# Sample attention as a chain of steps beside the prompt's weight tiles, and sixteen feed-forward tiles for the prompt alone

## The chip, the core and the metric

The kernel runs on one core of a Trainium2 chip. The core has a matrix engine (PE), whose weights are loaded by a second stream of instructions (PEld), a vector engine (DVE, VectorE), a scalar engine (ACT, ScalarE), a general engine (POOL, GpSimd) and SyncE (SP), which here only issues transfers. Each engine takes its instructions in the order of its own queue and waits on semaphores. Sixteen DMA engines carry the transfers that the queues of SP, ACT and POOL issue. PE writes its results to PSUM, eight banks of 128 x 512 float32, from where DVE or ACT fetch them; everything else lives in SBUF.

The metric is the time of one execution in microseconds (us) on the device. The kernel before was timed three times: 1074.62 us in the median, 1070.83 to 1075.09.

## The reference

One layer of a decoder handles a prompt of 512 rows and, with the same weights, 32 rows of samples (8 sequences of 4 new tokens), all of 1024 features in float32:

```python
h = rmsnorm(x, norm_mix_g)
q, k, v, qi, ki, wi, xl, gl, ga, gb = split_cols(h @ w_in, IN_SPLITS)
y_a = attend(q, k, v, qi, ki, wi) @ w_proj_a          # 8 heads of 64
y_b = (rg_lru(conv(xl)) * gelu(gl)) @ w_proj_b
x = x + (sigmoid(ga) * y_a + sigmoid(gb) * y_b) @ w_out
h = rmsnorm(x, norm_ffn_g)
ua, ub = split_cols(h @ w_up, (D_FF, D_FF))           # D_FF = 3072
uc = causal_dwconv(ua, width 3)
x = x + (gelu(uc) * ub) @ w_down
```

`attend` for a sample row scores 4096 past positions with a small indexer, takes the best 256, and attends to those alone: their keys and values (2 KB a row each) lie in a paged cache, so that each of the 32 rows gathers 256 rows of keys and 256 of values, at places that are known only at run time. The softmax also takes in the new tokens of the same sequence. Outputs are the normed rows, new keys and values, and states.

## The kernel before, in words

*Precision and weights.* Products that need it are made of float32r pairs: `load_w` (L162) loads a weight tile of 512 KB on SP's queue into one of three buffers `wr`; ACT makes the high half `wh` (L167), DVE the low half `wl` (L168), two buffers of each. A product then is three matmuls, high with high, low with high, high with low.

*The order of the work.* The program is written as a list; a planner with its own simulated timeline puts it into one queue for each engine. `tc.high_priority(n)` moves a part ahead in its choice, and `tc.issue_after(x)` allows an instruction only behind x. It is free otherwise, and the queues it makes are fixed: on the chip an instruction that waits holds all behind it in its engine's queue.

*Stages.* The first part, up to about 420 us, does the indexer, the recurrent block and the prompt's attention. Then come the choice of the samples' rows (L845 to L894), the projection of the prompt's attention (`w_proj_a`, L990 to L1010) and `w_out` (L1019 to L1044). The choice writes `idx`, the lists of 2 x 128 cache rows for each of the 32 sample rows.

*The feed-forward part for the prompt alone* (L1247 to L1265). D_FF is cut into 24 tiles of 128. The first NP = 12 are computed for the prompt's 512 columns alone with `form_p` (L253): two products (for `ua` and `ub`) of 24 matmuls of 512 columns each, the convolution on DVE, gelu on ACT, the halves `Gh` and `Gl`. After each four tiles `form_a` (L215) adds their part of `w_down`: 2 x 48 matmuls of 512 columns.

*The samples' attention* (L1059 to L1222) stands beside it in the list, at a priority of its own, so that the planner mixes both. `gather` (L1059) issues two indirect transfers of 256 KB on POOL's queue for a sample row, behind the last norm (`normed`); there are six buffers `cg` for them. Three ways turn 256 keys into scores, by a letter in `WAYS` (L147): with D (17 rows) DVE multiplies by the broadcast query (L1118; the query comes by an ACT-issued transfer of 256 KB) and sums in groups of 64 (L1125); with A (5 rows) DVE multiplies and ACT sums by 16 instructions (L1122); with P (10 rows) PE turns the keys by eight transposes (L1100), ACT copies them out of PSUM (L1101), and sixteen matmuls for two rows at a time (L1109) make the products. Then `softmax` (L1128) for 16 rows at a time, `values` (L1169) for four rows at a time (sixteen matmuls of 32 x 512, L1174), and `fold`, which sums them into `yrows`. After all, the samples' `w_proj_a`, gates, `w_out` and norm follow (L1207 to L1237), with loads on SP's queue.

*The feed-forward part for prompt and samples* (L1340 to L1372). The other 12 tiles are computed with `form_b` (L241) for 544 columns, as 24 matmuls of 256 and 24 of 288. Beside them `sample_steps` (L1289) does the samples' part of the first NP tiles, one step after each tile: `rows_by_columns` (L263) loads 512 columns of `w_up` again and makes bursts of 32 small matmuls (L278), one group for four tiles and each of `ua` and `ub`, then the same for `w_down`. At the end come the last `w_down` products (L1428 to L1430) and the final norms.

Of the kernel before, what the change touches and what calls it, by code (L numbers as in the profile page):

```python
# [9 lines left out]
F32 = mybir.dt.float32  # L10
# [8 lines left out]
D = 1024  # L19
# [9 lines left out]
NP = 12  # L29
# [67 lines left out]
def build(tc, I, O, dbg=None, mark=lambda n: None):  # L97
# [16 lines left out]
    with outer:  # L114
# [32 lines left out]
        WAYS = "PDDPPDDPDDDPADAPDDDPDAAPDDAPDDDP"  # L147
# [67 lines left out]
        def form_a(w, nk, a_hi, a_lo, a_s, col0, ncol, kc):  # L215
# [5 lines left out]
            for k0 in range(0, nk, kc):  # L221
# [7 lines left out]
                for t in range(4):  # L229
                    sl = slice(t * 128, (t + 1) * 128)  # L230
                    for k in range(kc):
                        kk = k0 + k
                        T.matmul(out[t], a_hi[:, kk, sl], hi[:, k, :], start=kk == 0, stop=False)  # L233
                        T.matmul(out[t], a_hi[:, kk, sl], lo[:, k, :], start=False, stop=False)  # L234
                        T.matmul(out[t], a_lo[:, kk, sl], hi[:, k, :], start=False, stop=kk == nk - 1)  # L235
# [17 lines left out]
        def form_p(w, col0, a_hi, a_lo, ps, first=None):  # L253
# [3 lines left out]
            for k in range(8):  # L257
                T.matmul(b, hi[:, k, :], a_hi[:, k, :SEQ], start=k == 0, stop=False)  # L258
                T.matmul(b, hi[:, k, :], a_lo[:, k, :SEQ], start=False, stop=False)  # L259
                T.matmul(b, lo[:, k, :], a_hi[:, k, :SEQ], start=False, stop=k == 7)  # L260
            return b

        def rows_by_columns(a_s, nk, mk, w, col0, burst):  # L263
# [3 lines left out]
            for k0 in range(0, nk, burst):  # L267
                rows = []
                for k in range(k0, k0 + burst, 2):
                    raw = mk((128, 2, 512))  # L270
                    nc.sync.dma_start(raw, w[k * 128:(k + 2) * 128, col0:col0 + 512].rearrange("(k p) c -> p k c", p=128))
                    rows += [raw[:, 0], raw[:, 1]]
                order = list(range(k0, k0 + burst))[::-1]
                head = None
                for k in order:
                    for c in range(4):
                        with tc.issue_after(head.ins) if head else ExitStack():
                            m = T.matmul(b[32 * c:32 * c + 32, :128], a_s[:, k, :], rows[k - k0][:, c * 128:(c + 1) * 128],  # L278
                                         start=k0 == 0 and k == order[0], stop=k0 + burst == nk and k == order[-1],
                                         tile_position=(0, 32 * c))  # L280
                        head = head or m
# [121 lines left out]
        kih = mp.tile([128, SEQ], F32R, name="kih")  # L403
# [434 lines left out]
        with tc.high_priority(PRIO // 10):  # L838
# [15 lines left out]
            scr2 = CW((128, 512), F16)  # L854
            for h4 in range(2):
# [5 lines left out]
                for t in range(4):  # L861
# [3 lines left out]
                    for j in range(2):  # L865
                        for bi in range(4):
                            T.matmul(bs[j][:, bi * 128:(bi + 1) * 128], oh[32 * t:32 * t + 32, bi, j * 128:(j + 1) * 128],
                                     M[32 * t:32 * t + 32, h4 * 4 + bi, 0:128], start=True, stop=True, tile_position=(32 * t, 0))
# [9 lines left out]
                    V.scalar_tensor_tensor(ix, phys, float(PG), slot, op0=ALU.mult, op1=ALU.add)  # L878

            vms = CW((128, 2, 288), BF16)  # L880
            selc = SM4((128, 4))
            V.tensor_copy(selc[96:128], sel[96:128, 1024:1028])
            for g in range(2):
                b = PC()
                T.matmul(b[:, 0:1], C("qh", g * 128, g * 128 + 128), cs_, start=True, stop=True)
# [8 lines left out]
                V.tensor_scalar(nw, nw, 1.0, BIG, op0=ALU.subtract, op1=ALU.mult)  # L894
        with tc.high_priority(PRIO // 3):
# [93 lines left out]
        with tc.high_priority(3 * PRIO):  # L989
# [7 lines left out]
            for ft in range(8):  # L997
# [6 lines left out]
                for k in range(4):  # L1004
                    T.matmul(b, hi[:, k, :], yahi[:, k, :], start=k == 0, stop=False)
                    T.matmul(b, hi[:, k, :], yalo[:, k, :], start=False, stop=False)
                    T.matmul(b, lo[:, k, :], yahi[:, k, :], start=False, stop=k == 3)
                V.scalar_tensor_tensor(sg, sg, 1.0, b, op0=ALU.add, op1=ALU.mult)
                V.tensor_tensor(sg, sg, zb, op=ALU.add)
                split_act(mhi[:, ft, :SEQ], mlo[:, ft, :SEQ], sg, 0.5)  # L1010
        xa = qp.tile([128, 2, D], F32, tag="q", name="xa")
# [5 lines left out]
        with tc.high_priority(PRIO // 3):  # L1017
            for c in range(2):
# [9 lines left out]
                for ks in ((0, 2), (2, 4), (4, 6), (6, 8)) if c == 0 else ((0, 8),):  # L1028
                    for t in range(4):
                        sl = slice(t * 128, (t + 1) * 128)  # L1030
                        for kk in range(*ks):
                            T.matmul(out[t], mhi[:, kk, sl], his[kk], start=kk == 0, stop=False)
                            T.matmul(out[t], mhi[:, kk, sl], los[kk], start=False, stop=False)
                            T.matmul(out[t], mlo[:, kk, sl], his[kk], start=False, stop=kk == 7)
# [7 lines left out]
                for t in range(4):  # L1042
                    o = x2[t][:, c * 512:(c + 1) * 512]
                    V.tensor_tensor(o, out[t], o, op=ALU.add)  # L1044
        h2hi, h2lo = mhi, mlo
        w_up, w_dn = I["w_up"][0], I["w_down"][0]

        with tc.high_priority(2 * PRIO):
            first = [columns(w_up, 8, c) for c in (0, DFF)]
            yn = mp.tile([128, 2, D], F32, tag="y3", name="yn")  # L1050
            for t in range(4):
                to_features(norm_rows(x2[t], 128, g2, lambda s: yn[:, t % 2]), t, h2hi, h2lo, None, PA)
            normed = powers[-1]

        with tc.high_priority(PRIO // 10):
            kc = I["cache_k"][0].rearrange("n s h d -> (n s) (h d)")
            vc = I["cache_v"][0].rearrange("n s h d -> (n s) (h d)")

            def gather(src, q, mk=None):  # L1059
                if mk is None:  # L1060
                    kt = CG((128, 2, 512))
                    kt = [kt[:, 0, :], kt[:, 1, :]], kt
                else:
                    kt = [mk(), mk()], None
                for j in range(2):
                    with tc.issue_after(normed.ins):
                        G.indirect_dma_start(out=kt[0][j], out_offset=None, in_=src,  # L1067
                                             in_offset=IndirectOffsetOnAxis(ap=idx[q // 16, q % 4][:, j, q // 4 % 4:q // 4 % 4 + 1], axis=0))
                return kt


            qbd = []
# [7 lines left out]
            junk = cp.tile([128, 64], F16, name="junk")  # L1080
            sTP = mp.tile([128, 1024], F32, tag="krs", name="sTP")
            sT = sTP[:, :512].rearrange("p (g j q h) -> p g j q h", g=2, j=2, q=16)
            V.memset(sTP, 0.0)
            sP = [sTP[:, 512 + g * 256:768 + g * 256] for g in range(2)]
# [385 lines left out]
```

## Time and profile before

| | us |
|---|---|
| timed, median of 3 | 1074.62 |
| the profiled execution | 1077.11 |
| its span, first to last instruction | 1075.0 |
| PE busy / DVE busy / ACT busy / POOL busy | 1007.3 / 695.9 / 425.4 / 187.9 |
| start of the stage with prompt tiles and sample attention | 516 |
| start of the stage for prompt and samples | 822 |
| last matmul ends | 1067.4 |

One execution is profiled, of 19144 instructions. Columns of a row of a group are: line, engine, operation, tile written and tiles read, shapes, count; then busy time and mean nanoseconds of one; then the idle time of the engine just before them and what ended it. A busy PE is not PE at its peak: matmuls overlap in the pipeline, and the distance between the starts of neighbours tells what one costs. PEclk is the clock that was granted to PE, as a share of full speed.

### The profile page before, as it was taken

Reading aid. Unit: us, or ns where it says so; the run is one execution under the profiler, and the core shown is the slowest. Engines: PE = TensorE matmul, PEld = TensorE weight load, DVE = VectorE, ACT = ScalarE, POOL = GpSimd, SP = SyncE. Lnnn points to the kernel's source line nnn. Section 1 sums busy time; section 2 is a strip of 40 time slices with the busy share of each in tenths; the row PEclk is TensorE's granted clock in tenths of the full one; section 3 lists DMA queues with packets and bytes.
Section 4 is the critical chain, followed back from the end, with each engine's and each line's share of the span. In section 5 each row is a group of like instructions: output and inputs, shape, how many; then the busy total and the mean of one; then the engine's idle time right before and its main releaser. Section 6 shows DMA issues by size and latency. Waiting matters only on the chain.

```text
span 1075.0 us, 19144 instructions
## 1 busy us (share of the span) xinstructions
PE 1007.3 (94%) x7516; PEld 825.3 (77%) x7516; DVE 695.9 (65%) x1517; ACT 425.4 (40%) x973; POOL 187.9 (17%) x183
## 2 busy tenths in 40 slices
PE   5999999999999997899789799869999999999997
PEld 4877988987788985677657576456688999999785
DVE  6655998999998857676668764333555454546352
ACT  5232654632365456343336643121332332324331
POOL 3420000001200000000568764635000000000000
PEclk9998999999999999799899899889999999999999
DMA  7751313336342334473488885755773776561401
GB/s 261 219 163 36 91 52 97 101 101 208 116 128 81 97 105 132 113 273 102 132 260 263 288 251 170 234 145 171 241 245 108 232 223 218 156 222 62 143 22 62
DMA packets 143141, 170.03 MB, mean 158 GB/s; under 512 B 12348, under 2 KB 94396, under 8 KB 143052
## 3 DMA queue, kind: packets, MB, share of 16 engines
q1 hardware_dynamic: 118952, 109.24, 33.1%
q0 software_dynamic: 12864, 42.75, 12.6%
q10 hardware_dynamic: 11236, 16.82, 5.0%
q8 instruction: 59, 0.97, 0.4%
q14 instruction: 30, 0.25, 0.1%
HBM read 159.10 MB, written 9.68 MB: 157 GB/s over the span
## 4 chain that ended last, share of the span: by engine, by line
PE 45%; DMA 5%; issue 4%; DVE 3%; POOL 1%; ACT 1%; another core or an unknown queue 1%; ACTq 0%; POOLq 0%; DVEq 0%; SPq 0%
DMA cg<-in_cache_k_dram,idx 2%; PE pd L233 2%; PE pd L235 2%; PE pd L234 2%; PE pc L278 2%; PE pa L248 2%; PE pa L250 2%; PE pd L248 2%; PE pa L249 2%; PE pd L249 2%; PE pd L250 2%; PE pa L258 1%; PE pd L258 1%; PE pa L259 1%; PE pa L260 1%
## 5 line engine op out<-in xcount | busy, mean ns | idle before, releaser
L167 ACT CAST wh<-wr 128x1024 fp32r<-128x1024 f32 (+1 forms) x124 | 123.0, 993 | 284.6 <-PE pd L235 67.8
L168 DVE TENSOR_TENSOR wl<-wr,wh 128x1024 fp32r<-128x1024 f32 (+1 forms) x124 | 143.1, 1154 | 132.9 <-ACT wh L167 119.8
L248 PE MATMUL pd<-hhi,wh 128*128 128x256 f32 (+1 forms) x384 | 114.4, 298 | 0.0
L250 PE MATMUL pd<-hhi,wl 128*128 128x256 f32 (+1 forms) x384 | 114.0, 297 | 0.0
L249 PE MATMUL pd<-hlo,wh 128*128 128x256 f32 (+1 forms) x384 | 112.5, 293 | 0.0
L176 POOL TENSOR_TENSOR smn<-smn,mhalf 128x1 f32<-128x1 f32 (+1 forms) x15 | 10.3, 687 | 460.8 <-DVE smn L1410 262.5
L1067 POOL DMA_INDIRECT cg<-in_cache_k_dram,idx x64 | 78.3, 1224 | 28.1 <-issue 15.8
L250 PEld LDWEIGHTS pd<-hhi,wl 128*128 128x128 f32 x384 | 72.8, 190 | 4.8 <-issue 3.2
L248 PEld LDWEIGHTS pd<-hhi,wh 128*128 128x128 f32 x384 | 72.8, 190 | 3.2 <-issue 1.9
L249 PEld LDWEIGHTS pd<-hlo,wh 128*128 128x128 f32 x384 | 72.9, 190 | 2.9 <-issue 2.5
L1067 POOL DMA_INDIRECT cg<-in_cache_v_dram,idx x48 | 50.0, 1041 | 28.5 <-issue 14.7
L377 POOL TENSOR_TENSOR pw<-pw,pw 128x512 f32<-128x512 f32 x8 | 11.2, 1397 | 198.4 <-DVE pw L374 197.0
L248 PE MATMUL pa<-mhi,wh 128*128 128x288 f32 (+1 forms) x144 | 42.2, 293 | 0.0
L250 PE MATMUL pa<-mhi,wl 128*128 128x288 f32 (+1 forms) x144 | 42.1, 293 | 0.0
L249 PE MATMUL pa<-mlo,wh 128*128 128x288 f32 (+1 forms) x144 | 42.1, 293 | 0.0
L248 PE MATMUL pd<-mhi,wh 128*128 128x256 f32 (+1 forms) x144 | 41.6, 290 | 0.0
L249 PE MATMUL pd<-mlo,wh 128*128 128x256 f32 (+1 forms) x144 | 41.4, 288 | 0.0
L250 PE MATMUL pd<-mhi,wl 128*128 128x256 f32 (+1 forms) x144 | 41.1, 288 | 0.0
L258 PE MATMUL pa<-mhi,wh 128*128 128x512 f32 x96 | 39.7, 413 | 0.0
L260 PE MATMUL pa<-mhi,wl 128*128 128x512 f32 x96 | 39.0, 406 | 0.4 <-issue 0.4
L259 PE MATMUL pd<-mlo,wh 128*128 128x512 f32 x96 | 38.9, 405 | 0.5 <-issue 0.5
L779 DVE MAX8 cw<-cg 128x8 f32<-128x1028 f32 x32 | 39.2, 1225 | 0.2
(604 smaller groups left out, 2831.1 us busy)
## 6 DMA issues: line engine op xcount, KB each, us to landing
wr<-in_w_up_dram SPq DMA_DIRECT2D x48, 512.0 KB
wr<-in_w_in_dram SPq DMA_DIRECT2D x36, 512.0 KB
sw<-in_w_up_dram SPq DMA_DIRECT2D x24, 512.0 KB
wr<-in_w_down_dram SPq DMA_DIRECT2D x18, 512.0 KB
cg<-in_w_in_dram SPq DMA_DIRECT2D x12, 512.0 KB
sw<-in_w_down_dram SPq DMA_DIRECT2D x12, 512.0 KB
xb<-qsd ACTq DMA_DIRECT2D x22, 256.0 KB
wr<-in_w_out_dram SPq DMA_DIRECT2D x8, 512.0 KB
```

Source lines behind the costliest of these rows:

```text
L167: S.copy(hi, raw)
L168: V.tensor_tensor(lo, raw, hi, op=ALU.subtract)
L233: T.matmul(out[t], a_hi[:, kk, sl], hi[:, k, :], start=kk == 0, stop=False)
L234: T.matmul(out[t], a_hi[:, kk, sl], lo[:, k, :], start=False, stop=False)
L248: T.matmul(b, hi[:, k, :], a_hi[:, k, c0:c1], start=k == 0, stop=False)
L249: T.matmul(b, hi[:, k, :], a_lo[:, k, c0:c1], start=False, stop=False)
L250: T.matmul(b, lo[:, k, :], a_hi[:, k, c0:c1], start=False, stop=k == nk - 1)
L258: T.matmul(b, hi[:, k, :], a_hi[:, k, :SEQ], start=k == 0, stop=False)
L259: T.matmul(b, hi[:, k, :], a_lo[:, k, :SEQ], start=False, stop=False)
L260: T.matmul(b, lo[:, k, :], a_hi[:, k, :SEQ], start=False, stop=k == 7)
L779: V.max(top[:, 8 * r:8 * r + 8], src)
L1067: G.indirect_dma_start(out=kt[0][j], out_offset=None, in_=src, in_offset=IndirectOffsetOnAxis(ap=idx[q // 16, q % 4][:, j, q // 4 % 4:q // ...
```

## The change

The key products on PE go: all 32 rows are multiplied on DVE, and every third (10) is summed on ACT, the others (22) on DVE. `sTP` with its part for PE products becomes `sT`.

The sample attention is no longer a free list beside the tiles but a generator, `sample_chain`, of 44 steps. The first asks for the rows of six sample rows ahead of the second norm; of the other 43 one is taken at each `next(chain)` in the prompt's loop: two for a tile and two after each half of `w_down`, 12 for four tiles, 48 in all. Each step's first instruction on PE, DVE or ACT stands behind (`behind`) the last one that the prompt's tile put on that engine (`turn`). Steps 1 to 13 hold the first sixteen rows' keys, one or two at a step; steps 13 to 29 the others, with values 0 to 2 among them; steps 30 to 41 the second softmax and the other values; steps 41 to 44 `w_proj_a`, `w_out` and the norm. Gathers are asked for as buffers come free (a row of keys takes one of six, four rows of values take three). The loads of the samples' `w_proj_a`, gates and `w_out` move to POOL's queue.

The choice of rows is a generator too, `choose`, of nine steps: four beside the last four tiles of the prompt's `w_proj_a`, the others beside the first half of `w_out`.

NP goes from 12 to 16, so that 16 tiles are done for the prompt alone and 8 for 544 columns, and the samples' groups for those grow from three to four. The first tile's products are made in two halves of 256 columns. The low half `Gl` and the copy `Gh` are written out singly.

```diff
-NP = 12
+NP = 16
...
-        WAYS = "PDDPPDDPDDDPADAPDDDPDAAPDDAPDDDP"
...
-        def form_p(w, col0, a_hi, a_lo, ps, first=None):
+        def form_p(w, col0, a_hi, a_lo, ps, first=None, halves=False):
...
+            for c0, c1 in ((0, 256), (256, 512)) if halves else ((0, SEQ),):
+                for k in range(8):
+                    T.matmul(b[:, c0:c1], hi[:, k, :], a_hi[:, k, c0:c1], start=k == 0, stop=False)
+                    T.matmul(b[:, c0:c1], hi[:, k, :], a_lo[:, k, c0:c1], start=False, stop=False)
+                    newest[0] = T.matmul(b[:, c0:c1], lo[:, k, :], a_hi[:, k, c0:c1], start=False, stop=k == 7)
...
+        def behind(eng):
+
+            return tc.issue_after(turn[eng].ins) if eng in turn else ExitStack()
+
+        def choose():
...
-                            T.matmul(bs[j][:, bi * 128:(bi + 1) * 128], oh[32 * t:32 * t + 32, bi, j * 128:(j + 1) * 128],
-                                     M[32 * t:32 * t + 32, h4 * 4 + bi, 0:128], start=True, stop=True, tile_position=(32 * t, 0))
+                            with behind("T"):
+                                T.matmul(bs[j][:, bi * 128:(bi + 1) * 128], oh[32 * t:32 * t + 32, bi, j * 128:(j + 1) * 128],
+                                         M[32 * t:32 * t + 32, h4 * 4 + bi, 0:128], start=True, stop=True, tile_position=(32 * t, 0))
...
-                    with tc.issue_after(normed.ins):
-                        G.indirect_dma_start(out=kt[0][j], out_offset=None, in_=src,
-                                             in_offset=IndirectOffsetOnAxis(ap=idx[q // 16, q % 4][:, j, q // 4 % 4:q // 4 % 4 + 1], axis=0))
...
+        def gather(dst, src, q):
+            for j in range(2):
+                G.indirect_dma_start(out=dst[j], out_offset=None, in_=src,
+                                     in_offset=IndirectOffsetOnAxis(ap=idx[q // 16, q % 4][:, j, q // 4 % 4:q // 4 % 4 + 1], axis=0))
...
+        def key_scores(q, kt, qb, act):
+            g, q16 = q // 16, q % 16
+            with behind("V"):
                 V.tensor_tensor(kt, kt, qb[:, None, :].to_broadcast([128, 2, 512]), op=ALU.mult)
-                if way == "A":
-                    for j in range(2):
-                        for h in range(8):
+            if act:
+                for j in range(2):
+                    for h in range(8):
+                        with behind("A"):
                             S.activation(junk, kt[:, j, h * 64:(h + 1) * 64], AF.Copy,
                                          accum_out=sT[:, g, j, q16, h:h + 1])
-                else:
+            else:
+                with behind("V"):
                     V.tensor_reduce(sT[:, g, :, q16, :], kt.rearrange("p j (h d) -> p j h d", h=8), axis=AX.X,
                                     op=ALU.add)
...
+            asked, room = [], 6
+            left = iter(turns)
+            cost = {"K": 1, "V": 3}
+            nxt = next(left)
+
+            def ask():
+                nonlocal nxt, room
+                while nxt and cost[nxt[0]] <= room and sum(k == "V" for (k, _), _ in asked) < 2:
+                    room -= cost[nxt[0]]
+                    asked.append((nxt, fetch(*nxt)))
+                    nxt = next(left, None)
...
+            while asked:
+                (kind, n), rows = asked.pop(0)
+                if kind == "K":
+                    done += 1
+                    nq = query(qs[done]) if done < 32 else None
+                    key_scores(n, rows, qb, done % 3 == 0)
+                    qb = nq
+                    if done % 16 == 0:
+                        g = done // 16 - 1
+                        side += [softmax(g), new_keys(g)]
+                else:
+                    while side:
+                        spare()
+                        yield
+                    side.append(values(n, rows))
+                    spare()
+                room += cost[kind]
+                ask()
+                if kind == "V" or (done % 4 if done < 17 else done % 4 != 2):
+                    yield
+                    spare()
...
-                b = rows_by_columns(ms, 8, CG, w_out, c * 512, 8)
+                b = rows_by_columns(ms, 8, CG, w_out, c * 512, 4, behind("T"), nc.gpsimd)
...
-                pa = form_p(w_up, ft * 128, h2hi, h2lo, PD, None if ft else first[0])
-                ub = form_p(w_up, DFF + ft * 128, h2hi, h2lo, PA, None if ft else first[1])
+                pa = form_p(w_up, ft * 128, h2hi, h2lo, PD, None if ft else first[0], ft == 0)
+                turn["T"] = newest[0]
...
                 gated_up(ft, fl, Gh, Gl, xb, uc)
-                S.activation(uc, uc, AF.Gelu_apprx_tanh)
+                next(chain, None)
+                ub = form_p(w_up, DFF + ft * 128, h2hi, h2lo, PA, None if ft else first[1], ft == 0)
+                turn["T"] = newest[0]
+                turn["A"] = S.activation(uc, uc, AF.Gelu_apprx_tanh)
                 V.tensor_tensor(uc, uc, ub, op=ALU.mult)
-                split_act(Gh[:, fl], Gl[:, fl], uc)
+                S.copy(Gh[:, fl], uc)
+                turn["V"] = V.tensor_tensor(Gl[:, fl], uc, Gh[:, fl], op=ALU.subtract)
+                next(chain, None)
...
+                for _ in range(n // 2):
+                    next(chain, None)
+        for _ in chain:
+            pass
```

More of the change, by code (lines that the diff above doesn't have):

```diff
@@ L1033, in build @@
                             T.matmul(out[t], mhi[:, kk, sl], los[kk], start=False, stop=False)
-                            T.matmul(out[t], mlo[:, kk, sl], his[kk], start=False, stop=kk == 7)
+                            turn["T"] = T.matmul(out[t], mlo[:, kk, sl], his[kk], start=False, stop=kk == 7)
+                    if c == 0:
+                        with tc.high_priority(PRIO // 10 - PRIO // 3):
+                            next(chosen, None)
                 if c == 0:
@@ new lines, in softmax, with fold @@
+            T.transpose(b[:32, 256:384], p[:, 256:288], ident)
+            S.copy(pT[:, g], b[:, :256].rearrange("p (j c) -> p j c", j=2))
+            S.copy(pTn[:, g, :], b[:32, 256:384])
+            yield
+        def fold(b, selm, first):
+            ym = CW()
+            V.tensor_tensor(ym, b, C("mh"), op=ALU.mult)
+            yield
+            b2 = PC()[:, :128]
+            head = None
+            for c in range(4):
+                with tc.issue_after(head.ins) if head else behind("T"):
+                    m = T.matmul(b2[32 * c:32 * c + 32], selm, ym[:, c * 128:(c + 1) * 128], start=True, stop=True,
+                                 tile_position=(0, 32 * c))
+                head = head or m
+            if first:
+                V.tensor_copy(yrows, b2)
+            else:
+                V.tensor_tensor(yrows, yrows, b2, op=ALU.add)
@@ new lines, in values, with column @@
+        def values(g8, vts):
+            b = PC()
+            def column(c, j):
+                return T.matmul(b[32 * c:32 * c + 32, :], pT[:, g8 // 4, j, (g8 % 4) * 32:(g8 % 4 + 1) * 32], vts[c][j],
+                                start=j == 1, stop=j == 0, tile_position=(0, 32 * c))
+            with behind("T"):
+                head = column(3, 1)
+            with tc.issue_after(head.ins):
+                for c, j in ((0, 1), (1, 1), (2, 1), (3, 0), (0, 0), (1, 0), (2, 0)):
+                    column(c, j)
+            yield from fold(b, C("sel", g8 * 32, g8 * 32 + 32), False)
@@ L1232, in build @@
                     V.scalar_tensor_tensor(o, b[32 * cc:32 * cc + 32, :128], 0.5, o, op0=ALU.mult, op1=ALU.add)
+            yield
+            y = norm_rows(x2[4], NQ, g2, CG)
+            yield
             h2s = hp.tile([128, 8, NQ], F32, tag="hs", name="h2s")
-            to_features(norm_rows(x2[4], NQ, g2, CG), 4, h2hi, h2lo, h2s, PC)
+            samples.append(h2s)
+            to_features(y, 4, h2hi, h2lo, h2s, PC)
+        samples = []
+        chain = sample_chain()
+        with tc.high_priority(PRIO // 10):
+            next(chain)
+        with tc.high_priority(2 * PRIO):
+            first = [columns(w_up, 8, c) for c in (0, DFF)]
+            yn = mp.tile([128, 2, D], F32, tag="y3", name="yn")
+            for t in range(4):
+                to_features(norm_rows(x2[t], 128, g2, lambda s: yn[:, t % 2]), t, h2hi, h2lo, None, PA)
         fsp = hp.tile([128, NP, 2], F32, name="fsp")
@@ L1292, in sample_steps @@
             for base, dst in ((0, xs4), (DFF, Gs1)):
[L1293 to L1294 removed]
+                for f4 in [*range(0, NP - 3, 4)] + [NP - 4] * (NP % 4 > 0):
+                    b = rows_by_columns(h2s, 8, SW, w_up, base + f4 * 128, 4, None)
                     rows = FT((128, 128))
```

285 lines of the change are left out of this document (130 added, 155 removed).

## Prediction

> **What bounds the kernel now.** I read the page first, for the span and the 40 slices; then the busy times by stage, with the stages cut where the feed-forward tiles for the prompt begin (516) and end (822); then the groups of that stage by line, and the timeline for the real spacing of matmuls, since a busy PE there is a pipelined one.
>
> ```profile
> span 1075.0 us, 19144 instructions
> PE 1007.3 (94%) x7516; PEld 825.3 (77%) x7516; DVE 695.9 (65%) x1517; ACT 425.4 (40%) x973; POOL 187.9 (17%) x183
> PE   5999999999999997899789799869999999999997
> GB/s 261 219 163 36 91 52 97 101 101 208 116 128 81 97 105 132 113 273 102 132 260 263 288 251 170 234 145 171 241 245 108 232 223 218 156 222 62 143 22 62
> ```
>
> ```profile
> core 0: us, PE busy (x) PEld busy (x) DVE busy (x) ACT busy (x) POOL busy (x), PEclk, DMA share, GB/s
> 420.00:516.00 96.00, 88.22 (x411) 66.49 (x412) 67.96 (x202) 40.42 (x118) 1.27 (x3) 0.91 0.49 154
> 516.00:650.00 134.00, 114.34 (x535) 85.81 (x535) 94.04 (x128) 66.91 (x221) 90.51 (x76) 0.91 0.77 240
> 650.00:720.00 70.00, 56.69 (x292) 37.67 (x291) 22.98 (x44) 15.86 (x22) 38.92 (x40) 0.88 0.67 201
> 720.00:822.00 102.00, 101.56 (x651) 74.09 (x651) 51.17 (x87) 25.80 (x36) 15.79 (x15) 1.00 0.62 194
> 516.00:822.00 306.00, 272.60 (x1474) 197.57 (x1475) 168.18 (x258) 108.58 (x279) 145.22 (x131) 0.93 0.69 216
> 822.00:1067.40 245.40, 244.55 (x2234) 221.18 (x2222) 115.41 (x265) 75.04 (x148) 2.19 (x4) 1.00 0.47 150
> ```
>
> PE is the bound. The stage 822 to 1067 has under 1 us of idle PE and the full clock: only less PE work shortens it. The stage 516 to 822, where twelve prompt tiles and the whole sample attention run side by side, has 306.0 - 272.6 = 33.4 us idle, and its granted clock is 0.93. All of that lies before 720, while keys and values are gathered; after 720 PE is full at clock 1.00. What ended the idle time there:
>
> ```profile
> L1174 PE MATMUL pc<-cg,cw 128*32 128x512 f32 x96 | 17.4, 652 | 4.4 <-DMA cg<-in_cache_v_dram,idx 4.4
> L1100 PE MATMUL pc<-cst,cg 128*128 128x128 f32 x80 | 13.1, 297 | 6.0 <-ACT ft L1101 5.1 <-DMA cg<-in_cache_k_dram,idx 0.9
> L1109 PE MATMUL pc<-ft,cw 128*32 128x256 f32 x80 | 10.8, 383 | 0.5 <-ACT pw L1258 0.5
> L234 PE MATMUL pa<-wl,Gp 128*128 128x512 f32 x24 | 10.7, 446 | 6.5 <-DVE wl L168 6.4
> L203 PE MATMUL pa<-cst,yn 128*128 128x128 f32 x24 | 4.1, 326 | 4.8 <-DVE yn L193 4.8
> L1133 PE MATMUL pc<-kTn,cw 128*128 128x32 f32 x16 | 2.6, 246 | 8.6 <-issue 8.6
> ```
>
> No single wait: the transposes of keys (L1100) wait for their copies, a weight half waits for VectorE, a value product for its gather, the second softmax (L1133) for nothing shown.
>
> **The change part by part.** First the prices on PE, from starts of neighbours in the timeline: an up-projection matmul of 512 columns; form_b's of 256 and 288; eight key transposes, sixteen key products and one burst of 32 sample matmuls, each with the next full-width starts behind it.
>
> ```profile
> 741.46 0.39 PE L259 MATMUL pd<-mlo,wh 128*128 128x512 f32 x1
> ...
> 746.38 0.40 PE L259 MATMUL pd<-mlo,wh 128*128 128x512 f32 x1
> ```
>
> ```profile
> 872.26 0.28 PE L249 MATMUL pc<-mlo,wh 128*128 128x256 f32 x1
> ...
> 874.83 0.28 PE L250 MATMUL pc<-mhi,wl 128*128 128x256 f32 x1
> ...
> 875.30 0.29 PE L248 MATMUL pc<-mhi,wh 128*128 128x288 f32 x1
> ...
> 878.39 0.30 PE L250 MATMUL pc<-mhi,wl 128*128 128x288 f32 x1
> ```
>
> ```profile
> 533.43 1.03 PE L1100 MATMUL pc<-cst,cg 128*128 128x128 f32 x8
> ...
> 534.54 0.40 PE L258 MATMUL pd<-mhi,wh 128*128 128x512 f32 x1
> ```
>
> ```profile
> 563.21 1.92 PE L1109 MATMUL pc<-ft,cw 128*32 128x256 f32 x16
> ...
> 565.40 0.40 PE L259 MATMUL pd<-mlo,wh 128*128 128x512 f32 x1
> ```
>
> ```profile
> 851.00 0.28 PE L249 MATMUL pd<-mlo,wh 128*128 128x256 f32 x1
> 851.21 1.08 PE L278 MATMUL pc<-sw,h2s 128*32 128x128 f32 x32
> ...
> 852.45 0.29 PE L248 MATMUL pd<-mhi,wh 128*128 128x288 f32 x1
> ```
>
> ```profile
> L227 PE MATMUL pc<-wr,Gs 128*32 128x128 f32 x96 | 4.3, 279 | 0.0
> L1421 PE MATMUL pc<-ft,Gs 128*32 128x128 f32 x64 | 2.0, 274 | 0.0
> ```
>
> (1) *Key products leave PE.* 21 starts of 512 columns take 4.92 us, 0.234 each. Eight transposes and the next matmul take 1.11 - 0.23 = 0.88; ten queries, 8.8 us. Sixteen products: 2.19 - 0.23 = 1.96, about 2.04 with the gap ahead of them; five pairs, 10.2. Together -19.0 us.
>
> (2) *Four tiles move.* form_b: 22 intervals in 2.57 us (0.117) and 23 in 3.09 (0.134), so 24 x 0.251 = 6.03 a call, 12.05 a tile: -48.2. form_p: 48 x 0.234 = 11.25 a tile: +45.0. Their 96 down-projection matmuls have the same width in both places: 0.
>
> (3) *Their sample part* becomes six more bursts of 32 (four for w_up, two for w_down): 1.45 - 0.24 = 1.21 each, +7.3; a third of L227 and L1421 goes, (4.3 + 2.0) / 3 = -2.1. Net +5.2.
>
> (4) *Choice of rows (L867) in steps behind the prompt's matmuls.* PE no longer waits for the one-hots:
>
> ```profile
> L867 PE MATMUL pc<-cw,cw 32*128 32x128 f16 x64 | 6.6, 220 | 2.4 <-DVE cw L860 2.2
> ```
>
> -2 (bounds -2.4 and, if the earlier gathers, 3.1 MB beside w_out's loads, delay a cast of w_out, +5). Gathers no longer wait for the last norm, so the first six keys land before the stage.
>
> (5) *The gaps.* -33.4 idle, and of the clock 306 x 0.07 = 21 us, part of it in the idle time itself; I take -15 (bounds -10 and -21). New ones come back, and no row shows them. They go by four prices:
>
> ```profile
> L1118 DVE TENSOR_TENSOR cg<-cg,xb 128x1024 f32<-128x1024 f32 x22 | 26.8, 1220 | 18.4 <-DMA cg<-in_cache_k_dram,idx 17.9 <-issue 0.2
> L1125 DVE TENSOR_REDUCE sTP<-cg 128x16 f32<-128x1024 f32 x17 | 20.6, 1212 | 0.1
> L1122 ACT ACTIVATE junk<-cg 128x64 f16<-128x64 f32 x80 | 20.5, 256 | 6.4 <-DVE cg L1118 2.9 <-issue 1.0 <-ACT pw L1255 0.5
> L1122 ACT ACTIVATION_READ_ACCUMULATOR junk<-cg 128x1 f32 x80 | 15.0, 187 | 0.0
> L1067 POOL DMA_INDIRECT cg<-in_cache_k_dram,idx x64 | 78.3, 1224 | 28.1 <-issue 15.8 <-DVE sTP L1125 8.9 <-remote 1.6
> ```
>
> Key work grows on VectorE from 22 products and 17 sums to 32 and 22 (+12.2, +6.1 us), on ScalarE from 5 to 10 queries of 16 x 0.443 = 7.1 us. Neither is a term of the sum: PE's own work of the new stage is 306 - 33.4 - 15 - 19.0 + 45.0 + 22.5 = 306 us, and 168.2 + 18 and 108.6 + 35 us lie beside it; without that cover they would cost those 18 and 35 us. Before, the 32 queries were pressed into 516 to 650; the chain takes them in 29 of its 44 steps, and 12 steps lie beside four tiles, 4 x 11.25 + 22.5 = 67.5 us, some 73 with the sample's own matmuls, 6 us a step, 175 us in all.
>
> Bytes: gathers 33.6 MB, w_up 16.8, w_down 8.4, queries 32 x 0.26 = 8.4, w_proj_a and w_out for the sample 6.3: 73.5 MB, 240 GB/s over 306 us, against 216 before. In the 16 steps that hold the second sixteen keys and four values: 8.4 + 4.2 + 8.4 + 8.4 = 29.4 MB in 100 us, 294 GB/s. The fastest slice of the page has 288, the key stage 240: 2 to 22 us too long. Buffered gathers and values that are used later spread it; I take 10. Each step now waits in its engine's order: a key product whose rows are late has the next weight halves queued behind it on VectorE, and PE waits for those (6.4 before; bounds 0 and the 17.9 that VectorE lost): 5. A value product or transpose that is late has the next tile's 24 matmuls behind it; the 4.4 of before for that lies in the 10. The second softmax: 0 to 8.6, 4. The first tile in halves starts after two norms (4.8 before): 1. That is 20 us, and with the clock that follows an idle PE, at before's rate of 15 for 33.4, +29.
>
> (6) *The tail.* Eight tiles now carry eight sample groups, and the sample's down-projection comes with no form_b tile left to cover it: 16 loads of 0.5 MB through three buffers, before at about 5 us for the two of a burst.
>
> ```profile
> 951.22 5.04 DMA sw<-in_w_down_dram
> ```
>
> Eight bursts of 5 to 6 us are 40 to 48, beside 45 us of down-projection: 0 to 12, I take +5. The twelve loads of the sample's w_proj_a and w_out go from SP's queue to POOL's behind the last gathers; SP's weight loads stand behind nothing more, and what the sample waits there is covered by the last two tiles while the chain's 44 steps stay within the 48 places.
>
> Sum: 1075.0 - 19.0 - 48.2 + 45.0 + 5.2 - 2 - 33.4 - 15 + 29 + 5 = 1041.6. The profiled execution took 1077.1 us, 2.1 over its span; the median shown, 1074.6, is 2.5 under it. So 1041.2, say **1041**.
>
> **The rivals.**
> *A: the gaps nearly vanish.* For it: after 720 the same mixture runs with 0.4 us idle. Against: there no keys are left. With 5 for 29 and 2 for 5: 1014.
> *B: the saved PE time is given back.* The stage goes at the pace of transfers and VectorE, the removed key work was mostly filler beside gathers. Full 22 us in the middle and before's 6.4 + 8.6 + 4.4 elsewhere are 41 idle, 60 with the clock, 31 above the forecast: 1072. For it: 0.77 DMA share while PE was idle. Against: keys spread over 175 instead of 134 us. That the change doesn't do what it says belongs here: a step is only held back behind a tile, never pulled forward to it, so the planner may still bunch them.
> *C, slower: rows late on VectorE in order.* A key product whose rows are late holds every weight half behind it; PE has two halves in hand. L1118 lost 17.9 us in 22 products though the planner placed them freely. PE must lose 20 + (1074.6 - 1041) / 1.45 = 43 us before this is slower at all; 32 products late by 2 us each, 64 us, give 1041 + 44 x 1.45 = 1105. Against: six keys' buffers are asked five steps ahead.
> *D, slower: gathers bound by their issue on POOL.* All 128 stand beside two-input VectorE work. Their rows: 1.22 us, and 0.3 between; the longest:
>
> ```profile
> 573.78 2.71 POOL L1067 DMA_INDIRECT cg<-in_cache_k_dram,idx  x1 [0.30 <-issue]
> ```
>
> Were each 2.71 + 0.3, 128 of them are 385 us; the forecast's stage is 306 + 29 = 335: +50, 1091. It decides from 335 / 128 = 2.6 us each. The Trainium skill, "SBUF — State Buffer", section "Who interferes with whom", says that VectorE and GpSimd share a port pair that one instruction holds whole, and that descriptor generation starves meanwhile. Here VectorE was busy 94 of 134 us and the mean still stayed at 1.22, so the trace bears out little of it.
>
> **How the numbers follow.** Forecast 0.50, A 0.18, B 0.19, C 0.09, D 0.04. The forecast's own range is 1025 to 1060 (gaps 15 to 45); with A and most of B, 1014 to 1073. Within 0.5% of before (5.4 us, about what a measurement of this kernel can tell from no change) lies more than half of B: same 0.12; A, the forecast and the rest of B give faster, 0.75; C and D slower, 0.13.
>
> **What would show it.** No 128x128 transposes of gathered keys; the sixteen tiles from 514 to about 848, with some 20 us of idle PE and a clock above 0.95; the tail with its eight tiles about 193 us (253 before); the next stall where values 1 to 3 meet the last keys. Wrong: VectorE idle for key rows above 30 us, gathers above 2 us, or matmuls of w_down for the sample with PE idle before them after the last gated tile.

## The result, and the profile after

The changed kernel takes 1044.3 us (median; 1042.2 to 1050.7) beside 1072.7 us for the kernel before on the same chip (1069.1 to 1075.1). The ratio is 0.974, 95% interval 0.969 to 0.979: 28 us faster, 3 us over the forecast of 1041. The profiled execution, 1050.7 us with a span of 1048.8, was the longest of them; a second profile of the same kernel on another chip has a span of 1036.5. Both are used below.

The page of the changed kernel: the same rows as of before.

```profile
span 1048.8 us, 18947 instructions
PE 984.0 (94%) x7342; PEld 804.8 (77%) x7342; DVE 712.8 (68%) x1506; ACT 440.6 (42%) x1101; POOL 194.5 (19%) x197
PE   4999999999999999799899899899989999999586
PEclk9999999999999999999899999989999999999889
```

PE's share of the span is 94% before and after: PE still bounds it, with 23.3 us less of busy PE. The low slices near the end are new.

The busy times by stage, cut some 3 us after w_out begins (456), some 3 us into the first of form_b's tiles (844; its first matmul starts at 840.8) and where the last of those tiles ends (958); ahead of them before's stages with the same cuts.

```profile
466.00:825.00 359.00, 325.60 (x1733) 238.97 (x1733) 203.67 (x365) 129.26 (x334) 146.49 (x133) 0.94 0.66 206
825.00:990.00 165.00, 164.19 (x1696) 158.06 (x1695) 82.69 (x197) 49.48 (x100) 0.00 (x0) 1.00 0.59 187
990.00:1067.00 77.00, 77.00 (x506) 60.33 (x503) 30.82 (x64) 24.79 (x47) 2.19 (x4) 1.00 0.21 74
```

```profile
core 0: us, PE busy (x) PEld busy (x) DVE busy (x) ACT busy (x) POOL busy (x), PEclk, DMA share, GB/s
456.00:844.00 388.00, 372.21 (x1914) 282.07 (x1915) 251.93 (x446) 166.36 (x516) 151.34 (x147) 0.98 0.66 213
844.00:958.00 114.00, 112.27 (x1202) 106.71 (x1200) 55.07 (x129) 33.27 (x69) 0.00 (x0) 1.00 0.65 204
958.00:1041.00 83.00, 68.30 (x663) 52.80 (x662) 29.91 (x69) 21.25 (x42) 2.20 (x4) 0.88 0.48 163
```

The first of these stages, w_out and the prompt's tiles, grew by 29 us only, though it took in four tiles (67 us with their down-projection): its idle PE fell from 33.4 to 15.8 us and its clock rose from 0.94 to 0.98. The stage of form_b lost 51 us. The last stage, full before at clock 1.00, now has 14.7 us of idle PE at 0.88. Which lines wait there (PE's groups from 958 on):

```profile
L1514 PE MATMUL pd<-whi,Gh 128*128 128x512 f32 x32 | 12.7, 398 | 0.0
...
L281 PE MATMUL pc<-sw,Gs 128*32 128x128 f32 x256 | 11.4, 334 | 12.5 <-DMA sw<-in_w_down_dram 12.4
```

12.4 of the 14.7 us are the sample's down-projection (L281) waiting for its weights; the prompt's matmuls (L1514) wait for nothing. And in the stage of the tiles (PE's waits from 0 to 860, in us in total, times and longest, those between 456 and 844 among them; after that the groups of VectorE and POOL that the rivals C and D speak of):

```profile
PE pc L1178 <- issue: 3.5, 4, 1.5
...
PE pd L260 <- ACT wh L166: 2.9, 1, 2.9
PE pd L260 <- DVE xa L1346: 2.3, 1, 2.3
...
PE pa L232 <- ACT wh L166: 1.2, 1, 1.2
...
PE pc L1178 <- DMA cg<-in_cache_v_dram,idx: 0.9, 1, 0.9
```

```profile
L1122 DVE TENSOR_TENSOR cg<-cg,xb 128x1024 f32<-128x1024 f32 x32 | 38.5, 1221 | 4.2 <-DMA xb<-qsd 3.2 <-issue 0.9
```

```profile
L1095 POOL DMA_INDIRECT cg<-in_cache_k_dram,idx x64 | 69.1, 1080 | 153.0 <-DVE pw L1025 73.8 <-DVE sT L1131 50.1 <-issue 14.6
L1095 POOL DMA_INDIRECT cg<-in_cache_v_dram,idx x48 | 52.5, 1093 | 17.8 <-issue 12.8 <-ACT junk L1127 3.7 <-DVE sT L1131 1.0
```

Only 0.9 us of PE's wait is for gathered rows; VectorE lost 18.4 us ahead of 22 key products before and 4.2 ahead of 32 now, none of it for gathered keys; a gather holds POOL 1.08 us.

### The profile page after: what moved, and what is told of

Its sections match the earlier page's. It is cut to its first block, busy times and chain, and to the rows that moved or that the text cites. A ratio compares the mean times of both kernels' runs of the same rounds, so it can differ in the third digit from the quotient of the medians.

```text
span 1048.8 us, 18947 instructions
## 1 busy us (share of the span) xinstructions
PE 984.0 (94%) x7342; PEld 804.8 (77%) x7342; DVE 712.8 (68%) x1506; ACT 440.6 (42%) x1101; POOL 194.5 (19%) x197
## 4 chain that ended last, share of the span: by engine, by line
PE 44%; DMA 7%; DVE 4%; ACT 2%; issue 2%; another core or an unknown queue 1%; POOL 0%; SPq 0%; ACTq 0%; POOLq 0%; DVEq 0%
PE pd L262 3%; PE pd L260 3%; PE pd L261 3%; PE pa L262 3%; PE pa L260 3%; PE pa L261 3%; PE pc L281 2%; DMA sw<-in_w_down_dram 2%; PE pc L1178 2%; PE pd L232 2%; PE pd L234 1%; PE pd L233 1%; DMA sw<-in_w_up_dram 1%; PE pa L247 1%; PE pa L248 1%
## 5 line engine op out<-in xcount | busy, mean ns | idle before, releaser
L1095 POOL DMA_INDIRECT cg<-in_cache_k_dram,idx x64 | 69.1, 1080 | 153.0 <-DVE pw L1025 73.8
L260 PE MATMUL pd<-mhi,wh 128*128 128x512 f32 (+1 forms) x136 | 54.4, 400 | 6.0 <-ACT wh L166 2.9
L262 PE MATMUL pa<-mhi,wl 128*128 128x512 f32 (+1 forms) x136 | 53.3, 392 | 1.1 <-issue 1.0
L261 PE MATMUL pd<-mlo,wh 128*128 128x512 f32 (+1 forms) x136 | 53.6, 394 | 0.3 <-DVE smn L176 0.3
L260 PE MATMUL pa<-mhi,wh 128*128 128x512 f32 (+1 forms) x136 | 52.8, 388 | 0.9 <-DVE mlo L154 0.9
L262 PE MATMUL pd<-mhi,wl 128*128 128x512 f32 (+1 forms) x136 | 53.5, 393 | 0.0
L261 PE MATMUL pa<-mlo,wh 128*128 128x512 f32 (+1 forms) x136 | 52.5, 386 | 0.1
L1127 ACT ACTIVATE junk<-cg 128x64 f16<-128x64 f32 x160 | 40.9, 256 | 23.1 <-issue 12.7
L1122 DVE TENSOR_TENSOR cg<-cg,xb 128x1024 f32<-128x1024 f32 x32 | 38.5, 1221 | 4.2 <-DMA xb<-qsd 3.2
L260 PEld LDWEIGHTS pd<-mhi,wh 128*128 128x128 f32 x136 | 26.9, 198 | 15.6 <-ACT wh L166 3.8
```

What stands on the lines that cost most here:

```text
L260: T.matmul(b[:, c0:c1], hi[:, k, :], a_hi[:, k, c0:c1], start=k == 0, stop=False)
L261: T.matmul(b[:, c0:c1], hi[:, k, :], a_lo[:, k, c0:c1], start=False, stop=False)
L262: newest[0] = T.matmul(b[:, c0:c1], lo[:, k, :], a_hi[:, k, c0:c1], start=False, stop=k == 7)
L1095: G.indirect_dma_start(out=dst[j], out_offset=None, in_=src, in_offset=IndirectOffsetOnAxis(ap=idx[q // 16, q % 4][:, j, q // 4 % 4:q // 4 ...
L1122: V.tensor_tensor(kt, kt, qb[:, None, :].to_broadcast([128, 2, 512]), op=ALU.mult)
L1127: S.activation(junk, kt[:, j, h * 64:(h + 1) * 64], AF.Copy, accum_out=sT[:, g, j, q16, h:h + 1])
```

## The experiments

Ratios are to the kernel before on the same chip, and times in the text are ratios times 1073.6 us, its median beside the last of the runs.

| version | ratio | 95% interval |
|---|---|---|
| changed kernel, first; again | 0.974; 0.970 | 0.969 to 0.979; 0.966 to 0.974 |
| before, keys off PE | 0.996 | 0.991 to 1.000 |
| before, sixteen tiles | 1.018 | 1.011 to 1.026 |
| changed, twelve tiles | 0.986 | 0.979 to 0.994 |
| changed, steps not held | 1.009 | 1.005 to 1.012 |
| changed, choice late | 0.983 | 0.980 to 0.986 |
| changed, one query's row | 0.979 | 0.972 to 0.986 |
| changed, six weight buffers; again | 0.950; 0.958 | 0.942 to 0.959; 0.954 to 0.962 |
| six buffers, two steps behind every second tile | 0.960 | 0.954 to 0.967 |
| six buffers, two steps behind the last three | 0.960 | 0.956 to 0.965 |
| six buffers, half the sums on ScalarE | 0.966 | 0.962 to 0.969 |

**The parts alone.** The kernel before without key products on PE, step (1):

```diff
-        WAYS = "PDDPPDDPDDDPADAPDDDPDAAPDDAPDDDP"
+        WAYS = "DADDDDADADDADADDDDADADDADADDDDAD"
```

> The kernel before with one part of the change: no query's keys go to PE; every third of the 32 queries is summed on ScalarE, the others on VectorE, in the free order of before. Theory F (the prediction's step 1: 19.0 us of PE work go, with the 5.1 us that PE waited for the copies of turned keys): 24 us less than before, about 1049. Rival B (that work was filler beside gathers, and VectorE with 18 us and ScalarE with 35 us more in the same 130 us take it back): within 6 us of before, 1067 to 1079, with more idle PE between 516 and 650 than before's 19.7 us.

Ratio 0.996, 5 us (0 to 10) for 19 us of removed PE work; PE's busy time is 14.6 us less (1007.3 to 992.7). In the stage of w_out and the prompt's tiles (458 to 820 here), idle PE rose from 33.4 to 40.6 us and the clock fell from 0.94 to 0.92. PE's largest waits there:

```profile
PE pc L1174 <- DMA cg<-in_cache_v_dram,idx: 14.3, 3, 5.5
PE pc L1133 <- issue: 8.0, 6, 1.9
PE pa L258 <- ACT wh L167: 3.7, 1, 3.7
```

PE reaches the value products sooner and waits for their rows instead: rival B's mechanism, true of this step without the chain.

The kernel before with sixteen tiles for the prompt alone, steps (2), (3) and (6) without the chain:

```diff
-NP = 12
+NP = 16
```

> The kernel before with sixteen tiles for the prompt alone, nothing else changed. Theory F (steps 2, 3 and 6: -48.2 + 45.0 + 5.2, and a tail that waits for the sample's down-projection weights, 15 us in the profile of after): 2 to 17 us more than before, 1075 to 1090. Rival T (the moved tiles by themselves are the gain, since they give the sample attention more cover): 10 to 20 us less, 1053 to 1063.

Ratio 1.018: 20 us slower (12 to 28), where the sum's terms for these steps, -48.2 + 45.0 + 5.2 + 5, make +7. Its last stage:

```profile
1005.00:1085.00 80.00, 66.39 (x658) 51.87 (x657) 29.76 (x68) 21.29 (x42) 2.19 (x4) 0.89 0.48 165
```

13.6 us of idle PE at clock 0.89, where the kernel before has none.

The changed kernel with twelve tiles, the chain without the four tiles:

```diff
-NP = 16
+NP = 12
```

> The changed kernel with twelve tiles for the prompt alone, as before: 36 places for the chain's 44 steps, so that the last eight (values 4 to 7, w_proj_a, w_out, norm) stand after the tiles with no prompt matmul placed between them. Theory F (keys off PE and quiet gaps are the gain, the tiles are only cover for the last steps): the gain of the changed kernel minus what the eight steps wait uncovered, some 1.5 to 3 us each, plus 12 us that the tail gets back: 1040 to 1058. Rival T (the sixteen tiles carry the gain): 1065 to 1075.

Ratio 0.986, 15 us faster. The chain's 44 steps no longer fit beside the tiles; its rest stands behind the last of their down-projections, covered by no more than 24 matmuls of the first form_b tile:

```profile
458.00:750.00 292.00, 281.25 (x1316) 215.98 (x1317) 206.50 (x362) 143.82 (x484) 131.41 (x117) 0.97 0.69 216
750.00:810.00 60.00, 30.08 (x334) 15.76 (x332) 12.25 (x33) 3.86 (x8) 25.50 (x30) 0.69 0.70 229
```

30 of 60 us idle, at a clock of 0.69. Four more tiles cost 20 us without the chain and bring 13 to 17 with it (0.986 to 0.974 or 0.970): they are the cover of its last steps.

**What the order of the chain is worth.** Nothing held behind the tiles, and the choice's matmuls not behind those of w_proj_a and w_out either:

```diff
         def behind(eng):
-            return tc.issue_after(turn[eng].ins) if eng in turn else ExitStack()
+            return ExitStack()
```

> The changed kernel, but its chain's steps are not held behind the prompt's tiles: the wait of a sample instruction for the newest prompt instruction of its engine is left out, so the planner places it by priority and buffers alone. Theory H (the hold spreads the work): without it key products and gathers bunch as in the kernel before; idle PE from the end of w_out to the first form_b tile rises from 15.8 to 25-40 us, ratio to before 0.983-0.995 against 0.974 of the changed kernel. Theory P (rival: the buffers of the gathers, six keys ahead, spread it in any case, the hold does nothing): idle stays 12-20 us and the ratio 0.970-0.978.

Ratio 1.009, slower than before, and 37 to 41 us over the changed kernel: H in its sign, at well over its price. The place is not the middle but the start. The stretch from 509 to 560, first of the changed kernel, then of this one, and from 456 to 560 the key products on VectorE and the transposes of the norm on PE, again of this one:

```profile
509.00:560.00 51.00, 48.28 (x255) 41.24 (x256) 40.97 (x101) 26.36 (x93) 12.80 (x12) 0.93 0.38 118
```

```profile
509.00:560.00 51.00, 27.90 (x151) 25.37 (x151) 46.08 (x103) 33.37 (x173) 33.95 (x31) 0.60 0.69 218
```

```profile
L202 PE MATMUL pa<-cst,yn 128*128 128x128 f32 x32 | 7.8, 425 | 10.0 <-DVE yn L192 10.0
```

```profile
L1122 DVE TENSOR_TENSOR cg<-cg,xb 128x1024 f32<-128x1024 f32 x22 | 26.7, 1218 | 4.5 <-issue 2.4 <-DMA xb<-qsd 2.1
L1131 DVE TENSOR_REDUCE sT<-cg 128x16 f32<-128x1024 f32 x15 | 18.0, 1213 | 0.1
```

In the changed kernel the same group has 6 products (7.3 us) up to 560. Left free, VectorE took 22 products and 15 sums, 45 us, between 456 and 560, and PE stood 23 of the 51 us from 509 on idle at clock 0.60. By its waits there, 10.0 are for the norm's rows on VectorE, 5.4 for sums of keys on ScalarE (the first softmax now stands inside the first tile) and 4.4 for ScalarE's part of the choice. The key products spread over 187 us here (466.6 to 653.7) and over 181 in the changed kernel (531.9 to 712.7). So it is not the length of the spread that the hold gives, but that the norm and the first tile come ahead of it on each engine. How much of the 37 to 41 us is the choice's hold alone, no run tells.

The choice of rows in one piece after w_out instead of in nine steps:

```diff
-                if ft >= 4:
-                    with tc.high_priority(PRIO // 10 - 3 * PRIO):
-                        next(chosen, None)
...
-                    if c == 0:
-                        with tc.high_priority(PRIO // 10 - PRIO // 3):
-                            next(chosen, None)
```

> The changed kernel with the choice of rows made in one piece after w_out instead of in nine steps from w_proj_a's fifth tile on. Theory S (the steps' gain is real, about 4 us ahead of w_proj_a and up to 6 in w_out, as the trace of the changed kernel reads): first w_proj_a matmul at 424-428 us instead of 422, first gathers after 500 instead of 457 us, and the total 5-12 us longer, ratio 0.979-0.985. Theory Z (rival: the earlier start of w_proj_a is the planner's other order and one execution's luck; the gathers are early enough either way): ratio 0.971-0.977, first w_proj_a matmul still at 420-424 us.

Ratio 0.983, as S expected, 10 to 14 us over the changed kernel. But w_proj_a starts at 420.7 us, as Z expected: the earlier start in the changed kernel's trace (422.4 against 430.4) is none of this step's doing; with the stepwise choice it was 420.1 in one profile and 426.9 in another. The loss is where the choice now stands, between w_out and the first tile. 509 to 530 of this version, then of the changed kernel:

```profile
509.00:530.00 21.00, 14.21 (x83) 12.11 (x82) 8.67 (x41) 7.64 (x35) 14.12 (x14) 0.66 0.66 191
```

```profile
509.00:530.00 21.00, 18.29 (x120) 16.70 (x121) 14.47 (x66) 8.92 (x36) 1.09 (x2) 0.84 0.00 1
```

Over the whole stage, idle PE is 24.0 against 15.8 us and the clock 0.94 against 0.98.

**What the gaps in the middle are.** One query's row for all 32 products, so that the rows of the other 31 queries are not loaded and the scores are those of one query:

```diff
-                    nq = query(qs[done]) if done < 32 else None
+                    nq = qb
```

> The changed kernel with the first query's broadcast row used for all 32 key products: 31 loads of 0.26 MB, 8.1 MB, are left out of the stage (the scores of the other 31 queries are those of the first query and so not the reference's). Theory T (transfers set the idle time in the middle, the 10 us of the prediction): idle PE of the stage falls from 15.8 to 5-9 us, ratio to before 0.960-0.966. Theory E (rival: single engine waits, on ScalarE's halves and a value product's unexplained pause, are the rest; transfers are hidden): idle stays 13-18 us, ratio 0.971-0.977.

Ratio 0.979, not under the changed kernel; the stage moves 194 instead of 213 GB/s and has 17.2 us of idle PE against 15.8. Theory T falls by its own sign: with 8 MB less to move, the idle time is no shorter. This version's w_out and norm came out in another order too (PE waits 4.6 us for a half of w_proj_a and 4.9 for the norm, which the changed kernel doesn't), so it isn't read to the microsecond.

Six buffers, and every sixth query's sums on ScalarE instead of every third:

```diff
-                    key_scores(n, rows, qb, done % 3 == 0)
+                    key_scores(n, rows, qb, done % 6 == 0)
```

> Six buffers, and only every sixth query's sums on ScalarE instead of every third: 5 of 10 queries, 80 pairs of instructions, 35 us of ScalarE, go to VectorE as 5 sums of 1.21 us. Theory U (PE's waits for weight halves of ScalarE in the stage, 4.1 us in the changed kernel, and the clock that follows come from these sums in its order): 3-8 us under the version with six buffers alone. Theory X (rival: ScalarE has slack, those waits come from elsewhere, or VectorE's order takes over): within 3 us of it, or up to 5 above.

Ratio 0.966, 8 us over six buffers alone. Theory U falls, X holds in its sign, with more than its 5 us. There was little to win: the 4.1 us for ScalarE's halves stand in the changed kernel's first profile alone; its second has 1.2, six buffers alone 1.2 and this version 1.6. What it lost, PE waits for on VectorE (4.9 against at most 0.7 with six buffers alone) and in pauses without a cause in the profile:

```profile
PE pd L260 <- DVE xa L1346: 4.9, 2, 2.6
PE pc L1166 <- issue: 4.3, 6, 1.8
...
PE pa L260 <- ACT wh L166: 1.6, 1, 1.6
```

**The tail.** Six buffers for the sample's weight halves, first beside the parts and then beside the changed kernel:

```diff
-        SW = maker(pool(ffn, "sw", 3), "sw")
+        SW = maker(pool(ffn, "sw", 6), "sw")
```

> The changed kernel with six buffers instead of three for the sample's weight rows in the tail. Theory W (PE in the tail waits for loads because only one and a half bursts fit in the buffers; 14.1 us of idle there by the profile of after, and 76 us at a clock of 0.87): 8 to 15 us less than the changed kernel, about 1032. Rival D (the loads are late because the queue or the DMA engines are full): within 3 us of it, 1041 to 1047.

> The changed kernel again, on one chip with the three versions that have six buffers for the sample's weight halves, for a comparison of those with it. Theory W (three buffers cost the tail some 12 us, as the traces read: 82.4 us behind the last form_b tile with three, 69.8 with six): ratio to before 0.968-0.979, 8-18 us above the version that has only the six buffers. Theory V (rival: the difference between the traces is the chip and the execution): the two within 4 us.

> The changed kernel with six buffers instead of three for the sample's weight halves, once more beside the changed kernel. Theory W: ratio to before 0.950-0.962, at least 8 us under the changed kernel. Theory V: within 4 us of it.

0.950 in the first comparison, where its six runs took from 1020 to 1039 us. Side by side, 0.970 for the changed kernel and 0.958 with six buffers: 13 us, theory W, and the fastest version measured. PE's group and the last stage with six buffers:

```profile
L281 PE MATMUL pc<-sw,Gs 128*32 128x128 f32 x256 | 9.9, 311 | 7.3 <-DMA sw<-in_w_down_dram 7.3
```

```profile
944.00:1017.00 73.00, 65.52 (x671) 51.78 (x669) 30.06 (x70) 21.41 (x43) 2.20 (x4) 0.93 0.47 164
```

From the first form_b matmul to the end of the span it is 193.8 us, against 204.7 in the changed kernel's second profile; that matmul starts at 831.1 and 831.8, so the gain lies behind it.

Six buffers, and a second sample step behind every second of the eight tiles, so that the sample's down-projection lies beside form_b:

```diff
                 next(steps, None)
+                if fl % 2:
+                    next(steps, None)
```

> Six buffers instead of three for the sample's weight halves, and two sample steps instead of one behind every second of the eight gated tiles, so that the sample's down-projection lies beside form_b. Theory L (the tail waits because no form_b is left to cover the loads): idle PE after the last form_b tile falls from 6.1 us (six buffers alone) and 14.5 us (changed kernel) to under 2 us, ratio to before 0.940-0.948 on a chip where six buffers alone gave 0.950. Theory Q (rival: the queue that carries both the tiles' weights and these halves is the bound, so the wait only moves into the form_b tiles): idle after it falls but 4-10 us of idle appear between form_b tiles, ratio 0.948-0.956.

Ratio 0.960. The last stage is full (0.1 us idle, clock 1.00), but the wait stands one stage earlier, in this group between the first and the last form_b tile:

```profile
L281 PE MATMUL pc<-sw,h2s 128*32 128x128 f32 x478 | 16.0, 284 | 4.4 <-DMA sw<-in_w_up_dram 4.4
```

From the first form_b matmul to the end it is 193.1 us, 0.7 less than six buffers alone: theory Q by its idle time, though the ratio lies above the ranges of both (they were set beside the 0.950 of the first comparison). With the second step behind the last three tiles only (`if fl > 4`):

> Six buffers, and a second sample step behind only the last three of the eight gated tiles, so that the gating and both halves of the sample's down-projection are issued with those tiles and the loads of w_up for the earlier steps are not crowded (two steps behind every second tile left 4.4 us of waits for w_up between the form_b tiles). Theory L (there is room on the queue for the halves of w_down beside the last tiles): idle PE from the first form_b tile to the last matmul under 3 us, 3-6 us under the version with six buffers alone. Theory Q (rival: the queue is full there, the wait only moves): 4-8 us of idle in all, within 3 us of it.

Ratio 0.960, 4.5 us of idle there in all, 190.0 us to the end: theory Q again, no faster in the total. What is left of the tail can't be told from no change.

## Why the prediction was right, and where it was not

The total held partly by luck: two terms erred in opposite ways. Against the forecast's 848 us for the end of the prompt's tiles and 193 from there to the end, the first form_b matmul starts at 840.8 (second profile 831.8), and 208.0 (204.7) follow.

- *(1) -19.* The work left PE, 14.6 us of busy time when taken alone. Alone it brought 5 us; more came only with the chain and its order. The prediction's reason against rival B, keys spread over 175 us, is not what decided: without the hold they spread over 187 us and nothing is gained. What decided is that no step stands ahead of the prompt's work on its engine. The prediction gave that hold no price, and left open that the planner may bunch the steps all the same. It is worth 37 to 41 us, more than the whole gain.
- *(2), (3) and (6), +7 together.* Measured +20. The prices of the tiles need no correction to explain it: the tail is the term that was mis-sized. "Eight bursts of 5 to 6 us are 40 to 48, beside 45 us of down-projection: 0 to 12, I take +5" assumed that loads and matmuls overlap freely. With three buffers, two of which a burst holds, little is loaded ahead, and the idle PE is 13.8 to 14.7 us with the clock at 0.88 to 0.89. From the first form_b matmul on it took 208.0 us (second profile 204.7) for the 193 predicted, so the +5 was +17 to +20, over its upper bound of 12; with six buffers it is 193.8. One of the prediction's own signs of being wrong thus came: the sample's matmuls of w_down with PE idle before them.
- *(4) -2.* Its working failed: PE still waits for the one-hots in w_out, 5.0 us ahead of L878 against 2.4 ahead of L867 before.

```profile
L878 PE MATMUL pc<-cw,cw 32*128 32x128 f16 x52 | 5.6, 218 | 5.0 <-DVE cw L870 3.2 <-ACT slot L887 1.3 <-DVE slot L886 0.4
```

  What the step brings is 10 to 14 us after w_out, where the choice no longer stands ahead of the first tile; the prediction had named the earlier gathers without a price.
- *(5) -33.4 - 15 + 29.* Too much came back in the sum. Of the four prices, "I take 10" for transfers in the middle found next to nothing: PE waits 0.9 us for gathered rows, and the run with one query's row has no less idle time; the second softmax (L1138, L1140) had no wait for 4; the first tile in halves waited 2 us for 1; VectorE and ScalarE in order, 5, were 6.4 (2.3, 2.9 and 1.2; 1.9 in the second profile). What the prediction had no term for are pauses of PE ahead of value products, 3.5 us (second profile 5.1). Idle of 15.8 (second profile 12.5) against "some 20", clock 0.98 against "above 0.95". Steps (1), (4) and (5) together were -40.4 in the sum; the runs leave 28 + 20 = 48 for them (52 with the second comparison). With them the stage ended 7 us early (second profile 16), and the 15 (12) more that the tail took nearly cancel it. The split goes by one order of adding the parts: the four tiles cost 20 us without the chain and bring 13 to 17 with it.
- *The rivals.* A is refuted for the kernel as it is: even with six buffers 13.7 and 7.3 us of idle stay, and 0.958 is 1029, not 1014. B holds for step (1) alone. C and D did not come; 4.2 us of VectorE's idle and gathers of 1.08 us are far from the 43 us and 2.6 us from which they decide. The prediction's rule for D, from the Trainium skill, "SBUF — State Buffer", "Who interferes with whom", doesn't fit this work: the section ties the full block to VectorE's 2-port modes and says that tensor_tensor and tensor_reduce, the operations of the key products and sums here, didn't stall such transfers. The trace agrees: VectorE was busy 252 of 388 us and the gathers were shorter than before (1.08 against 1.22).

What isn't settled: which of the remaining 12 to 16 us of idle in the stage can be had, since taking sums from ScalarE made it longer, and why.

## What to carry to other kernels

Give the order of filler work a price of its own: in an engine's queue, ready filler placed ahead of a critical step cost more here (37 to 41 us) than all the PE work that the change removed. When cover moves from one stage to another, price the stage it leaves by its buffers, not by bytes against matmul time: with three buffers, transfers that fitted by duration still left 14 us of idle PE. Measure the parts alone as well as together; here one part brought 5 us, the other cost 20, and with the chain and its order they bring 28.

## What the runs showed of the hardware

*Pauses of PE without a cause.* In the changed kernel the sixteen matmuls of one value product took 9.4 us (765.46 to 774.83), where the sixteen that start at 757.58 took 1.9. The granted clock was 1.00 in both. PE's timeline, up to the last pause:

```profile
765.46 1.02 PE L1178 MATMUL pc<-cg,cw 128*32 128x512 f32 x2
766.07 0.60 PE L1178 MATMUL pc<-ft,cw 128*32 128x512 f32 x1
768.15 0.59 PE L1178 MATMUL pc<-ft,cw 128*32 128x512 f32 x1 [1.48 <-issue]
768.85 1.28 PE L1178 MATMUL pc<-cg,cw 128*32 128x512 f32 x2
770.95 1.02 PE L1178 MATMUL pc<-cg,cw 128*32 128x512 f32 x3 [0.82 <-issue]
772.35 0.59 PE L1178 MATMUL pc<-cg,cw 128*32 128x512 f32 x1 [0.38 <-issue]
773.75 0.59 PE L1178 MATMUL pc<-ft,cw 128*32 128x512 f32 x1 [0.81 <-issue]
```

It has the form of before's 8.6 us at the second softmax, now at another line, and POOL issues gathers every 1.25 us at the same time. But POOL issues them at that pace beside the quick group at 757.58 too, so the gathers alone don't make the pause. No run here tells what holds PE.

*The clock follows idle PE, and working matmuls pay for it.* Over whole stretches it was lower where PE was less busy, though not in strict order: 0.93 at 95% (509 to 560, changed kernel), 0.88 at 82% (its last stage), 0.69 at 50% (twelve tiles, 750 to 810), 0.60 at 55% (steps not held, 509 to 560). The version with twelve tiles shows the same value products ahead of a wait of 5.8 us, behind it, and later:

```profile
757.49 0.59 PE L1178 MATMUL pc<-ft,cw 128*32 128x512 f32 x1
...
765.98 1.06 PE L1178 MATMUL pc<-ft,cw 128*32 128x512 f32 x1
...
779.82 0.59 PE L1178 MATMUL pc<-ft,cw 128*32 128x512 f32 x1
```

The granted clock was 1.00 from 751 to 758, 0.50 from 765.9 to 769.5 with PE busy for 3.53 of 3.6 us, and 1.00 again from 779.8 to 781. So an idle stretch costs more than its own length here: the work behind it ran at half the clock for a while.
